# Slots of h of 2,304 bytes instead of 2,176, and two buffers instead of three for two working tiles

## The chip, the core and the metric

The kernel runs on one core of one Trainium2 chip. The metric is the device time of one execution in microseconds (us); times are given as the median of several executions. Engines are named as in the profile: PE (TensorE) multiplies, PEld is its loading of the stationary operand, DVE (VectorE) and ACT (ScalarE) work on elements, POOL (GpSimd) does little here, SP issues the transfers.

## What is computed

One block of a streaming encoder, for 256 frames of 2048 channels in float32: two half-step feed-forward layers (FFN, 5504 channels) around a mixer of attention and pooling, each conditioned on a vector c, then a last norm. Cut to what matters here:

```python
mod = silu(c) @ w_ada + b_ada                 # nine vectors of 2048
sh1, sc1, g1, sh2, sc2, g2, sh3, sc3, g3 = split(mod, 9)
h = rmsnorm(x, ffn1_norm_g) * (1 + sc1) + sh1
a, b = split(h @ ffn1_w_in, 2)
x = x + 0.5 * g1 * ((silu(a) * b) @ ffn1_w_out)
h = rmsnorm(x, mix_norm_g) * (1 + sc2) + sh2
q, k, v, f, u = split(h @ w_in, ...)
x = x + g2 * (concat(attention(q, k, v, f), pool(u)) @ w_out)
h = rmsnorm(x, ffn2_norm_g) * (1 + sc3) + sh3
a, b = split(h @ ffn2_w_in, 2)
x = x + 0.5 * g3 * ((silu(a) * b) @ ffn2_w_out)
return rmsnorm(x, final_norm_g)
```

## The kernel before, in words

Channels lie on the 128 partitions, frames along them: x is 16 tiles (k = 0 to 15) of 128 x 256. Each float32 operand of a product is split into a high and a low part of type fp32r, and a product is three matmuls, high x high, high x low, low x high. `mm3` issues them for one weight tile of 128 x 128: L242 (wh with the high half of h, g or mix), L243 (wh with the low half), L244 (wl with the high half). The weights are the loaded operand, 256 columns of h, g or mix the moving one. I call these three a triple. In the projections of q, k and v (`project`, L768) it is the other way round: h is loaded, and the weights move.

**Weights** come in pieces of eight tiles (`load_piece`: 512 KB, five buffers raw). ACT copies a piece to wh in two halves (L193, `split_high`), DVE subtracts to wl (L203, `split_low`); there are four wh and three wl buffers, in turn. The pieces' order is the order in which PE uses the tiles, and it is written out by `next_piece`, which for each piece also lets the work beside it go on by one step: it splits the next piece, loads one further, adds a rate to a credit (`RATE0`: 0.36 per piece for the first 50, then `RATE1`: 0.40 while scales and shifts of a norm are next, 0.33 otherwise) and, at a credit of 1, loads one of the 144 rows of w_ada (1 MB, L109), which DVE multiplies with silu(c) and sums (L112). Its `step_chains` takes one step of each chain put off with `later`.

**h.** `make_h` builds tile k of a norm's output: DVE writes x * a * row into a working tile hu (L307), ACT adds the shift and writes the high half of h (L311), DVE writes the low half from hu and the high one (L314). The tile is 128 x 2 x 256 elements, high half first. `make_raw` builds a tile hraw of x * a without the row, of 2 x 258 elements used out of 2 x 272, for the products that start before the norm's root is known: pool tiles 6 and 7 and the first three visits' halves of the second FFN (`raw_of`).

**Stages.** `ffn_in` goes over 43 pairs of output tiles in visits: a visit takes one pair and all h tiles that are ready and not yet used for it, one PSUM half after the other. The first visit of the second FFN takes three pairs (`GROUP`), with k outermost, so that 18 matmuls in a row read one h tile. `residual_out` multiplies g (43 tiles) or mix (16 tiles), and adds to x. Between the FFNs stand the pool tiles (`pool_tile`), the projections and the attention.

**Working tiles touched by the change**, all 128 x 256 float32 or less: the ring "hu" (hu, and guess and rest of a norm's root in `rms_row`), three buffers, and the ring "act" (sq in `Stats.add`, L272; silu in `swiglu`, L383; junk in `norm_heads`, L783), three buffers.

**Where the tiles lie.** The built program gives each tile an address in bytes within a partition. The ring "h" has 16 slots, each of the size of its largest tile, hraw: 2 x 272 x 4 = 2,176 bytes. Slot n begins at 29,440 + 2,176 n: for even n a multiple of 256, for odd n 128 beyond one. The low half of h lies 1,024 bytes further, with the same remainder. In the ring "h" also lie the squares at the start (sq4) and the outputs at the end (ys). The ring "pair" follows, from 64,256, with 43 slots of 2,048 bytes: g, mix, pooled, spill and the attention's tiles; all begin at a multiple of 256 (remainder 768 of 1,024). Then come ada, raw and the weight parts: their halves begin 64 bytes beyond a multiple of 256, but for one half of every fourth wh tile (128 beyond, `BEHIND`) and all of every third wl tile (192 beyond). In the first visit of the second FFN, k = 0 to 7 lie in slots 11, 10, 15, 14, 13, 9, 12 and 0.

The order of DVE, ACT, PE and SP is written by hand (`manual_schedule`): an engine does its instructions in the order in which the program issues them.

Of the kernel before, what the change touches and what calls it, by code (L numbers as in the profile page):

```python
# [10 lines left out]
F32 = mybir.dt.float32  # L11
F32R = mybir.dt.float32r
# [4 lines left out]
P = 128  # L17
SEQ = 256
# [5 lines left out]
HD = 128  # L24
# [23 lines left out]
NEG = -3.0e38  # L48
GAP = 16
BEHIND = {"wh": (0, 0, 0, 2 * GAP), "wl": (0, 0, 0)}  # L50
WARM = 9
QSCALE = float(HD) ** -0.5

# [12 lines left out]
def block_kernel(ctx, tc, order, xT, cvec, wada, wts, wf, vecs, out):  # L66
# [5 lines left out]
    big = ctx.enter_context(tc.tile_pool(name="big", bufs=1))  # L72
    wpool = ctx.enter_context(tc.tile_pool(name="wpool", bufs=1))
    work = ctx.enter_context(tc.tile_pool(name="work", bufs=2))
# [3 lines left out]
    def mm_tile():  # L78
        return psum.tile([P, 512], F32, tag="mm", name="mm", bufs=4)

    def sm_tile():
        return psum.tile([P, 512], F32, tag="sm", name="sm", bufs=4)

    def pair_tile(shape, dt, name):
        return big.tile(shape, dt, tag="pair", name=name, bufs=43)
# [55 lines left out]
    def later(*steps):  # L141
        chains.append(list(steps))

    def step_chains(most=None):

        if most is None:
            for c in chains:
                c.pop(0)()
            chains[:] = [c for c in chains if c]
        else:  # L150
            while len(chains) > most:
                for f in chains.pop(0):
                    f()
# [20 lines left out]
    def part_tile(kind):  # L174

        behind = BEHIND[kind]
        i = turns[kind] % len(behind)
# [69 lines left out]
    def inverse_root(r, v, n, guess, rest):  # L247


        def first():  # L250
            nc.scalar.activation(guess, v, AF.Abs_reciprocal_sqrt, scale=1.0 / n, bias=eps_t)

        def newton():
            nc.vector.scalar_tensor_tensor(out=rest, in0=v, scalar=n * EPS, in1=guess, op0=ALU.add, op1=ALU.mult)
            nc.vector.scalar_tensor_tensor(out=rest, in0=rest, scalar=-0.5 / n, in1=guess, op0=ALU.mult, op1=ALU.mult)
            nc.vector.scalar_tensor_tensor(out=r, in0=rest, scalar=1.5, in1=guess, op0=ALU.add, op1=ALU.mult)

        return first, newton

    class Stats:  # L260
# [6 lines left out]
        def add(self, d):  # L267
            t = {}

            def square():  # L270
                t["sq"] = work.tile([P, SEQ], F32, tag="act", name="sq", bufs=3)
                nc.scalar.activation(t["sq"], x[d], AF.Square)  # L272

            def total():
                if d == KD - 1:
                    self.last = t["sq"]
                elif self.acc is None:
                    self.acc = work.tile([P, SEQ], F32, tag="gf", name="acc", bufs=3)
                    nc.vector.tensor_copy(out=self.acc, in_=t["sq"])
                else:  # L280
                    nc.vector.tensor_add(out=self.acc, in0=self.acc, in1=t["sq"])

            later(square, total)
            if d == KD - 1:
                step_chains(0)

        def rms_row(self, meanwhile=None, between=None):

            st = sm_tile()
            parts = self.parts or (self.acc, self.last)  # L290
            for i, part in enumerate(parts):
                nc.tensor.matmul(st[:, :SEQ], lhsT=ones, rhs=part, start=i == 0, stop=i == len(parts) - 1)  # L292
            self.row = work.tile([P, SEQ], F32, tag="rrow", name="rrow", bufs=1)
            guess, rest = (work.tile([P, SEQ], F32, tag="hu", name=n, bufs=3) for n in ("guess", "rest"))
            first, newton = inverse_root(self.row, st[:, :SEQ], D, guess, rest)
            first()
            if between:
                between()
            newton()
            if meanwhile:  # L300
                meanwhile()
            return self.row

    def make_h(d, rrow, a_col, b_col):

        u = work.tile([P, SEQ], F32, tag="hu", name="hu", bufs=3)
        nc.vector.scalar_tensor_tensor(out=u, in0=x[d], scalar=a_col, in1=rrow, op0=ALU.mult, op1=ALU.mult)  # L307
        h = big.tile([P, 2, SEQ], F32R, tag="h", name="h", bufs=16)

        def high():  # L310
            nc.scalar.activation(h[:, 0, :], u, AF.Identity, bias=b_col)  # L311

        def low():
            nc.vector.scalar_tensor_tensor(  # L314
                out=h[:, 1, :], in0=u, scalar=b_col, in1=h[:, 0, :].bitcast(F32), op0=ALU.add, op1=ALU.subtract
            )

        return h, high, low

    def make_raw(d, a_col, b_col):  # L320

        h = big.tile([P, 2, SEQ + 16], F32R, tag="h", name="hraw", bufs=16)[:, :, : SEQ + 2]
        b2 = b_col.to_broadcast([P, 2])

        def high():
            nc.scalar.activation(h[:, 0, :SEQ], x[d], AF.Copy, scale=a_col)
            nc.scalar.copy(out=h[:, 0, SEQ:], in_=b2)

        def low():
            nc.vector.scalar_tensor_tensor(  # L330
                out=h[:, 1, :SEQ], in0=x[d], scalar=a_col, in1=h[:, 0, :SEQ].bitcast(F32),
                op0=ALU.mult, op1=ALU.subtract,
            )
            nc.vector.tensor_sub(out=h[:, 1, SEQ:], in0=b2, in1=h[:, 0, SEQ:].bitcast(F32))

        return h, high, low
# [40 lines left out]
    def swiglu(ab, j, g):  # L377

        t = {}

        def act():
            t["s"] = work.tile([P, SEQ], F32, tag="act", name="silu", bufs=3)
            nc.scalar.activation(t["s"], ab[:, :SEQ], AF.Silu)  # L383

        def product():
            t["g"] = work.tile([P, SEQ], F32, tag="gf", name="gf", bufs=3)
            nc.vector.tensor_mul(out=t["g"], in0=ab[:, SEQ:512], in1=t["s"])
            g[j] = pair_tile([P, 2, SEQ], F32R, f"g{j}")

        def high():  # L390
            nc.scalar.copy(out=g[j][:, 0, :], in_=t["g"])

        def low():
            nc.vector.tensor_sub(out=g[j][:, 1, :], in0=t["g"], in1=g[j][:, 0, :].bitcast(F32))

        return act, product, high, low
# [100 lines left out]
    def modulated(s_sc, s_sh, v_norm, rrow_of, n_raw=0):  # L497
# [5 lines left out]
        def begin_raw(k):  # L503
            c = slice(k, k + 1)
            raw_h[k], *steps = make_raw(k, scales[s_sc][:, c], shifts[s_sc][:, c])
            rest["raw", k] = steps
            later(lambda: go_on(("raw", k), 1), lambda: go_on(("raw", k), 0))
# [19 lines left out]
        def start(k, wait=True):  # L527
            c = slice(k, k + 1)
            begun_h[k], high, low = make_h(k, rrow_of(), scales[s_sc][:, c], shifts[s_sc][:, c])
            if wait:  # L530
                slow.add(k)
                rest[k] = [high, low]
                later(lambda: None, lambda: go_on(k, 1), lambda: go_on(k, 0))
            else:
                high()
                rest[k] = [low]
# [92 lines left out]
    idle = mm_tile()  # L629
    for _ in range(WARM):  # L630
        nc.tensor.matmul(idle[:, :SEQ], lhsT=ones, rhs=x[0], start=True, stop=True)
# [142 lines left out]
    def norm_heads(pts, name):  # L774
        qr = [pair_tile([P, 4, HD], F32, f"qr{name}{tt}") for tt in range(2)]
        ss = work.tile([P, 8], F32, tag="ss", name="ss")
        r, guess, rest = (work.tile([P, 8], F32, tag=n, name=n) for n in ("rs_r", "rs_guess", "rs_rest"))

        def squares(tt):
            nc.scalar.copy(out=qr[tt], in_=pts[tt].rearrange("p (a b) -> p a b", a=4))  # L780
            for i in range(4):
                junk = work.tile([P, HD], F32, tag="act", name="junk", bufs=3)
                nc.scalar.activation(  # L783
                    junk, qr[tt][:, i, :], AF.Square, accum_out=ss[:, tt * 4 + i : tt * 4 + i + 1]
                )

        def scale(tt):
            for i in range(4):
                nc.scalar.activation(
                    qr[tt][:, i, :], qr[tt][:, i, :], AF.Copy, scale=r[:, tt * 4 + i : tt * 4 + i + 1]  # L790
                )

        later(lambda: squares(0), lambda: squares(1), *inverse_root(r, ss, HD, guess, rest), lambda: scale(0), lambda: scale(1))
        return qr
# [300 lines left out]
```

## Time and profile before

| what | value |
|---|---|
| median of 3 runs | 1770.55 us (1770.16 to 1771.66) |
| the profiled execution | 1770.31 us, its span 1768.6 us |
| busy: PE, PEld | 1753.8 us (99%), 1743.8 us (99%) |
| busy: DVE, ACT | 1371.4 us (78%), 922.2 us (52%) |
| read from HBM | 476.24 MB, 270 GB/s over the span |
| first FFN, products with h | 19 to 504 us |
| first FFN, products with g | 504 to 740 us |
| pool tiles 6 and 7, projections, attention | 740 to 905 us |
| pool tiles with h, attention | 905 to 948 us |
| products with mix | 948 to 1038 us |
| second FFN, raw tiles, then h | 1040 to 1521 us |
| second FFN, products with g | 1521 to 1756 us |

The span runs from the first to the last instruction; the execution's own time lies 1.7 us above it. A matmul's duration in the rows is the time from its start to its modelled end; matmuls overlap, so their pace is the distance from start to start: for a line of code, its last start less its first, over its count less one. A slice of 50 us shows how many matmuls overlap it (x430), how long each engine was busy in it, the granted clock and what the DMA engines moved.

### The profile page before, as it was taken

What the parts mean: (1) busy time and instruction counts of PE and PEld (TensorE: products, weight loads), DVE (VectorE), ACT (ScalarE), POOL (GpSimd) and SP (SyncE); (2) the same over time, 40 slices, a digit from 0 to 9 for tenths busy, and PEclk for the clock granted to TensorE, in tenths of its full rate; (3) what the DMA queues carried; (4) which work ended last, traced back from release to release, by engine and by line L of the source; (5) the groups of instructions that cost most, each with busy time, mean ns of one, the idle gap of its engine ahead of it and who ended that gap; (6) DMA issues with size and microseconds to landing.
All of it is one profiled execution on the core that took longest, in us unless ns stands there. A gap on an engine that the chain in (4) does not pass through costs nothing.

```text
span 1768.6 us, 37313 instructions
## 1 busy us (share of the span) xinstructions
PE 1753.8 (99%) x14966; PEld 1743.8 (99%) x14966; DVE 1371.4 (78%) x2390; ACT 922.2 (52%) x1871; POOL 8.3 (0%) x54
## 2 busy tenths in 40 slices
PE   9999999999999999999999999999999999999997
PEld 7999999999999999999999999999999999999997
DVE  7899889999988888797989998777765555555554
ACT  7644445555554444477766555544444444544442
POOL 0000000000000000100000000000000000000000
PEclk9999999999999999999999999999999999999999
DMA  9889898888889989767966977877775555555553
GB/s 367 317 319 331 319 339 316 309 308 314 311 319 335 328 329 334 286 237 301 344 223 248 330 285 249 296 268 259 262 258 189 189 188 191 191 191 192 194 195 112
DMA packets 111937, 480.79 MB, mean 272 GB/s; under 512 B 12425, under 2 KB 12689, under 8 KB 93329
## 3 DMA queue, kind: packets, MB, share of 16 engines
q1 hardware_dynamic: 111762, 478.39, 75.4%
q8 instruction: 117, 1.92, 0.4%
q14 instruction: 58, 0.48, 0.1%
HBM read 476.24 MB, written 2.11 MB: 270 GB/s over the span
## 4 chain that ended last, share of the span: by engine, by line
PE 98%; ACT 1%; DMA 1%; DVE 0%; issue 0%; SPq 0%; DVEq 0%
PE mm L243 30%; PE mm L242 29%; PE mm L244 29%; PE mm L768 8%; DMA ada<-in_wada 1%; ACT wh L193 0%; ACT spill L454 0%; DVE y L1029 0%; PE sm L802 0%; PE sm L832 0%; PE sm L881 0%; PE sm L872 0%; PE sm L292 0%; PE sm L699 0%; PE sm L701 0%
## 5 line engine op out<-in xcount | busy, mean ns | idle before, releaser
L193 ACT CAST wh<-raw 128x512 fp32r<-128x512 f32 x1228 | 701.2, 620 | 725.1 <-PE mm L243 442.0
L203 DVE TENSOR_TENSOR wl<-raw,wh 128x512 fp32r<-128x512 f32 x1228 | 788.2, 686 | 319.0 <-issue 285.2
L242 PE MATMUL mm<-h,wh 128*128 128x256 f32 x2800 | 782.1, 279 | 0.8 <-ACT h L311 0.4
L243 PE MATMUL mm<-h,wh 128*128 128x256 f32 x2800 | 782.8, 280 | 0.1
L244 PE MATMUL mm<-h,wl 128*128 128x256 f32 x2800 | 781.9, 279 | 0.0
L242 PEld LDWEIGHTS mm<-h,wh 128*128 128x128 f32 x2800 | 526.3, 188 | 2.0 <-ACT spill L454 1.0
L243 PEld LDWEIGHTS mm<-h,wh 128*128 128x128 f32 x2800 | 525.8, 188 | 0.4 <-DVE h L314 0.3
L244 PEld LDWEIGHTS mm<-h,wl 128*128 128x128 f32 x2800 | 526.0, 188 | 0.0
L244 PE MATMUL mm<-g,wl 128*128 128x256 f32 x1376 | 380.8, 277 | 0.0
L243 PE MATMUL mm<-g,wh 128*128 128x256 f32 x1376 | 380.5, 277 | 0.0
L242 PE MATMUL mm<-g,wh 128*128 128x256 f32 x1376 | 380.5, 276 | 0.0
L112 DVE SCALAR_TENSOR_TENSOR ada<-ada,crow 128x2048 f32<-128x2048 f32 x144 | 329.2, 2286 | 23.5 <-DMA ada<-in_wada 22.9
L243 PEld LDWEIGHTS mm<-g,wh 128*128 128x128 f32 x1376 | 258.4, 188 | 0.0
L244 PEld LDWEIGHTS mm<-g,wl 128*128 128x128 f32 x1376 | 258.4, 188 | 0.0
L242 PEld LDWEIGHTS mm<-g,wh 128*128 128x128 f32 x1376 | 258.3, 188 | 0.0
L768 PE MATMUL mm<-wh,h 128*128 128x256 f32 x768 | 137.3, 282 | 0.0
L768 PEld LDWEIGHTS mm<-wh,h 128*128 128x128 f32 x768 | 117.4, 188 | 0.5 <-issue 0.2
L768 PE MATMUL mm<-wl,h 128*128 128x256 f32 x384 | 107.2, 279 | 0.0
L768 PEld LDWEIGHTS mm<-wl,h 128*128 128x128 f32 x384 | 72.3, 188 | 0.0
L244 PE MATMUL mm<-mix,wl 128*128 128x256 f32 x256 | 70.9, 277 | 0.0
L243 PE MATMUL mm<-mix,wh 128*128 128x256 f32 x256 | 70.8, 277 | 0.0
L242 PE MATMUL mm<-mix,wh 128*128 128x256 f32 x256 | 70.8, 277 | 0.0
(166 smaller groups left out, 1002.9 us busy)
## 6 DMA issues: line engine op xcount, KB each, us to landing
raw<-in_wts SPq DMA_DIRECT2D x614, 512.0 KB, 4.4
ada<-in_wada SPq DMA_DIRECT2D x144, 1024.0 KB, 7.6
x<-in_xT SPq DMA_DIRECT2D x4, 512.0 KB, 5.5
out<-y SPq DMA_DIRECT2D x8, 256.0 KB, 2.2
fb<-frow_d SPq DMA_DIRECT2D x4, 256.0 KB, 8.0
vec<-in_vecs SPq DMA_DIRECT2D x1, 109.5 KB, 10.1
wfc<-in_wf SPq DMA_DIRECT2D x1, 64.0 KB, 5.7
crow<-in_cvec SPq DMA_DIRECT2D x1, 8.0 KB
```

Source lines behind the costliest of these rows:

```text
L112: nc.vector.scalar_tensor_tensor(out=r, in0=r, scalar=1.0, in1=crow, op0=ALU.mult, op1=ALU.mult, accum_out=mod[section][:, t : t + 1],)
L193: nc.scalar.copy(out=wh[i], in_=raws[0][:, i * HALF : (i + 1) * HALF])
L203: nc.vector.tensor_sub(out=wl[i], in0=raw[:, i * HALF : (i + 1) * HALF], in1=wh[i].bitcast(F32))
L242: nc.tensor.matmul(out_ap, lhsT=wh, rhs=hk[:, 0, :], start=start, stop=False, skip_group_check=shared)
L243: nc.tensor.matmul(out_ap, lhsT=wh, rhs=hk[:, 1, :], start=False, stop=False, skip_group_check=shared)
L244: nc.tensor.matmul(out_ap, lhsT=wl, rhs=hk[:, 0, :], start=False, stop=stop, skip_group_check=shared)
L768: nc.tensor.matmul(pts[tt][:, c], lhsT=lhs, rhs=rhs[:, c], start=k == 0 and not half and not i, stop=k == KD - 1 and i == 2, skip_group_ch ...
```

## The change

`h_slot` gives every tile h and hraw the same room of 576 elements, 2,304 bytes, nine times 256. The low half of h stays 1,024 bytes behind the high one; that of hraw moves from 1,088 to 1,152 bytes behind it. The rings "hu" and "act" go from three buffers to two. Of the 16 x 128 bytes that the slots take more, and the 2 x 1,024 bytes that the two rings take less, nothing is left over.

```diff
+SLOT = 576
...
-                t["sq"] = work.tile([P, SEQ], F32, tag="act", name="sq", bufs=3)
+                t["sq"] = work.tile([P, SEQ], F32, tag="act", name="sq", bufs=2)
...
-            guess, rest = (work.tile([P, SEQ], F32, tag="hu", name=n, bufs=3) for n in ("guess", "rest"))
+            guess, rest = (work.tile([P, SEQ], F32, tag="hu", name=n, bufs=2) for n in ("guess", "rest"))
...
+    def h_slot(name, half):
+
+        return big.tile([P, SLOT], F32R, tag="h", name=name, bufs=16)[:, : 2 * half].rearrange("p (a b) -> p a b", a=2)
+
     def make_h(d, rrow, a_col, b_col):
 
-        u = work.tile([P, SEQ], F32, tag="hu", name="hu", bufs=3)
+        u = work.tile([P, SEQ], F32, tag="hu", name="hu", bufs=2)
         nc.vector.scalar_tensor_tensor(out=u, in0=x[d], scalar=a_col, in1=rrow, op0=ALU.mult, op1=ALU.mult)
-        h = big.tile([P, 2, SEQ], F32R, tag="h", name="h", bufs=16)
+        h = h_slot("h", SEQ)
...
     def make_raw(d, a_col, b_col):
 
-        h = big.tile([P, 2, SEQ + 16], F32R, tag="h", name="hraw", bufs=16)[:, :, : SEQ + 2]
+        h = h_slot("hraw", SEQ + P // 4)[:, :, : SEQ + 2]
...
-            t["s"] = work.tile([P, SEQ], F32, tag="act", name="silu", bufs=3)
+            t["s"] = work.tile([P, SEQ], F32, tag="act", name="silu", bufs=2)
...
-                junk = work.tile([P, HD], F32, tag="act", name="junk", bufs=3)
+                junk = work.tile([P, HD], F32, tag="act", name="junk", bufs=2)
```

In the built program slot n of "h" now begins at 29,440 + 2,304 n, a multiple of 256 for every n. "pair" begins at 66,304, and every tile behind it lies 2,048 bytes further than before, up to the end of the ring "act", behind which nothing moves. On every engine the instructions stand in the same order as before. What differs is what some wait for: 24 of the 48 writes of hu wait for a later instruction of DVE than before or for one at all, and 34 of ACT's on sq, silu and junk for one of ACT.

## Rows read from the trace of the kernel before

**Rows 1.** The page: busy time per engine, granted clock, chain that ended last.
```profile
PE 1753.8 (99%) x14966; PEld 1743.8 (99%) x14966; DVE 1371.4 (78%) x2390; ACT 922.2 (52%) x1871; POOL 8.3 (0%) x54
...
PEclk9999999999999999999999999999999999999999
...
PE 98%; ACT 1%; DMA 1%; DVE 0%; issue 0%; SPq 0%; DVEq 0%
```

**Rows 2.** PE's longest wait: <- releaser: us in total, times, longest.
```profile
PE mm L600 <- DMA crow<-in_cvec: 2.5, 1, 2.5
```

**Rows 3.** PE on h, two stretches: xcount: ns min/median/max, first and last start.
```profile
L242 PE MATMUL mm<-h,wh x1333: 276/279/290, 36.0 to 503.8; 128*128 128x256 f32 x191
...
L242 PE MATMUL mm<-h,wh x1328: 274/279/284, 1055.8 to 1520.9; 128*128 128x256 f32 x190
```

**Rows 4.** PE on tiles g (526:726) and mix (956:1036), the same view.
```profile
L242 PE MATMUL mm<-g,wh x586: 276/276/284, 525.8 to 725.8; 128*128 128x256 f32 x196
...
L244 PE MATMUL mm<-mix,wl x235: 276/276/285, 955.8 to 1035.8; 128*128 128x256 f32 x118
```

**Rows 5.** PE's timeline, second FFN's first visit: each slot's first matmul (start).
```profile
1057.90 0.28 PE L242 MATMUL mm<-h,wh 128*128 128x256 f32 x1
...
1059.95 0.28 PE L242 MATMUL mm<-h,wh 128*128 128x256 f32 x1
...
1062.04 0.28 PE L242 MATMUL mm<-h,wh 128*128 128x256 f32 x1
...
1064.16 0.28 PE L242 MATMUL mm<-h,wh 128*128 128x256 f32 x1
...
1066.31 0.28 PE L242 MATMUL mm<-h,wh 128*128 128x256 f32 x1
...
1068.43 0.28 PE L242 MATMUL mm<-h,wh 128*128 128x256 f32 x1
...
1070.55 0.28 PE L242 MATMUL mm<-h,wh 128*128 128x256 f32 x1
...
1072.66 0.28 PE L242 MATMUL mm<-h,wh 128*128 128x256 f32 x1
```

**Rows 6.** Timeline of PE where the stage of g begins.
```profile
504.46 0.28 PE L242 MATMUL mm<-g,wh 128*128 128x256 f32 x1
...
507.64 0.28 PE L242 MATMUL mm<-g,wh 128*128 128x256 f32 x1
...
508.67 0.28 PE L242 MATMUL mm<-g,wh 128*128 128x256 f32 x1
```

**Rows 7.** Stretches: us, busy PE, PEld, DVE, ACT, POOL (x), PEclk, DMA, GB/s.
```profile
76.00:126.00 50.00, 50.00 (x430) 50.00 (x429) 48.32 (x80) 22.41 (x41) 0.00 (x0) 1.00 0.90 319
...
226.00:276.00 50.00, 50.00 (x430) 50.00 (x429) 45.40 (x73) 24.65 (x45) 0.00 (x0) 1.00 0.92 333
526.00:576.00 50.00, 50.00 (x441) 50.00 (x440) 43.01 (x78) 23.43 (x46) 0.00 (x0) 1.00 0.92 333
```

**Rows 8.** DVE: ada from 226 to 276 us, hu, a piece of the chain.
```profile
L112 DVE SCALAR_TENSOR_TENSOR ada<-ada,crow 128x2048 f32<-128x2048 f32 x7 | 16.0, 2287 | 3.7 <-DMA ada<-in_wada 3.7
...
L307 DVE SCALAR_TENSOR_TENSOR hu<-x,a,rrow x48: 474/480/487, 18.2 to 1111.0; 128x256 f32<-128x256 f32 x48
...
1759.30 0.02 issue
1759.33 0.43 DVE rest L255
```

**Rows 9.** PE on h (904:948), on hraw, and line L768: xcount: ns.
```profile
L242 PE MATMUL mm<-h,wh x96: 276/279/467, 904.9 to 947.0; 128*128 128x256 f32 x96
...
L243 PE MATMUL mm<-hraw,wh x80: 279/283/386, 739.9 to 1055.5; 128*128 128x258 f32 x80
...
L768 PE MATMUL mm<-wh,h x768: 274/279/476, 752.3 to 904.7; 128*128 128x256 f32 x192
L768 PE MATMUL mm<-wl,h x384: 276/279/292, 752.5 to 904.8; 128*128 128x256 f32 x192
```

## The prediction

> **What bounds the kernel now.** I read the page's busy times first: PE is busy for 1753.8 of 1768.6 us, its granted clock is at its full level (2.4 GHz) in every slice, and the chain that ended last is PE for 98% [rows 1]. The list of PE's waits comes next: its longest entry is 2.5 us, once, at the start [rows 2]. So PE hardly ever waits for another engine, and only two things can move the time: the number of matmuls, which the change leaves alone, or the pace at which one matmul follows another. A triple is the three matmuls of one weight tile (L242, L243, L244, 256 columns each). Its pace follows from first start, last start and count of one line. In the first FFN's input stage 1333 triples take 467.8 us, 351.2 ns each; in the second FFN's, 1328 take 465.1 us, 350.5 ns [rows 3]. In the stages that read g and mix the same three instructions take 200.0 us for 585 intervals (g), or 80.0 us for 234 (mix), which is 341.9 ns [rows 4]. Shape, type, weights and clock are the same; h costs 8.6 to 9.3 ns more per triple. What differs is where the moving operand starts: all g and mix tiles begin at a multiple of 256 bytes, of h every second slot begins 128 bytes beyond one.
>
> **Does the address make the difference?** The first visit of the second FFN keeps one h tile for 18 matmuls, slot after slot [rows 5]. Slot 10 (even, aligned) takes 2.05 us, 342 ns per triple. Slot 15 takes 2.09, slot 13 takes 2.15, slot 9 takes 2.12 us (odd; 348, 358 and 353 ns). But slots 14, 12 and 0 (even) take 2.12, 2.12 and 2.11 us, the slow pace too. So there are two paces, about 342 and about 353 ns per triple, and an aligned operand allows the fast one without forcing it. The stage of g shows how a slow stretch ends. It inherits the slow pace from h: the first nine triples of g take 3.18 us, 353 ns each, then three take 1.03 us [rows 6], and from 526 us on the average is 341.9 [rows 4]. Nothing else happened there than that aligned tiles followed each other over several weight pieces. With h as it is, an odd slot comes after almost every even one, so the slow pace is renewed each time; 351 is what a mixture of 342 and 353 or more gives.
>
> The Trainium skill speaks against this change. Its page TensorE: Matmul & The Clock Gate (Part 2: What happens when you issue a matmul) says that the moving operand and the weight load have independent read ports, so that loading the next weights takes nothing from the running matmul, and gives a gap of N/2.4 + 2.5 ns. By that an estimate from the page is 109 ns per matmul, 328 ns per triple, at any address, and the change would be worth nothing. The rows disagree: 350.5 and 341.9 ns for equal instructions at one clock [rows 3, 4].
>
> **The change, part by part.**
> 1. Slots of 2,304 bytes from the same first address: every h tile then starts at a multiple of 256, its low half 1,024 further, also a multiple. I take the pace of g and mix for h, as the row of the same instructions on tiles that are all aligned. First FFN: 1333 x (351.2 - 341.9) = 12.4 us. Second: 1328 x (350.5 - 341.9) = 11.4 us. The six later pool tiles have 96 triples of h [rows 9]; at 8.6 ns that is 0.8 us. Sum 24.6 us, all on PE and so on the path. Bounds: upward 24.6 us, since no stage of the trace runs this triple faster than 341.9; downward a loss, in the rivals.
> 2. Slow stretches that remain after PE has waited or after the raw tiles: the one of rows 6 lasted nine triples at 11 ns, 0.1 us. I allow six of them, 0.6 us.
> 3. The cover. With PE faster, DVE has less time for each weight piece. Between 76 and 126 us it is busy for 48.3 of 50 us; the same pieces at 341.9 instead of 351.2 would come in 48.7 us, so it just fits. From 226 to 276 us it is busy for 45.4, with DMA at a share of 0.92 and 333 GB/s [rows 7], and waits 3.7 us for rows of ada [rows 8]. In the stage of g DMA had the same share and rate, at the faster pace of PE [rows 7]. But in the stage of h the rate of ada is 0.40 per piece once 50 pieces are through, against 0.36, so some waits may reach PE: between 0 and half of the first FFN's gain, 6 us. I take 1 us, since the wl tiles are made ahead by up to two pieces and the next stage ran at that pace without a wait.
> 4. Two buffers for hu. The instructions of every engine keep their order; only waits differ. 24 of the 48 writes of hu (480 ns each [rows 8]) now wait for a later instruction of DVE itself, nearly always the last before them that read the old tile. Such a wait on its own engine shows as the 0.02 us of "issue" between the dependent instructions of the last root [rows 8]: 24 x 0.02 = 0.5 us of DVE, beside PE. Queued behind are splits of weights, covered as in 3. If that cover were gone it would be 0.5 us on the path; I take 0.
> 5. Two buffers for sq, silu and junk. 34 instructions of ACT get or change a wait on ACT itself, at the same price 0.7 us of an engine that is busy for 52% [rows 1]: 0.
> 6. The raw tiles: their low half now starts 1,152 bytes behind the high one, 128 beyond a multiple of 256, while the high half is aligned. 80 triples [rows 9] at plus or minus 11 ns are within 0.9 us; before, none of their low halves was aligned either. I take 0.
> 7. The projections (L768) have the weights as moving operand, at addresses that keep their remainder, and h as the loaded one. Of 1152 matmuls [rows 9] half load an odd slot; bounds are 0 and 576 x 11/3 ns = 2.1 us. I take 0, since the moving side doesn't change.
> All that lies behind the h slots moves by 2,048 bytes, eight times 256, which costs nothing.
> Sum: 24.6 - 0.6 - 1.0 = 23.0 us. The profiled execution took 1770.31 us (the median of the runs is 0.24 us higher): **1747.3 us**.
>
> **The rivals.**
> *Only the odd slots gain.* They come to what an even slot gives today, and the even ones stay. With odd triples at 353 [rows 5] and a mean of 350.9 over both stages, even ones stand at 348.8; with 354 they stand at 347.8. 1400 odd triples times 4.2 to 6.2 ns is 6 to 9 us: 1762 to 1764 us. For it: slots 12 and 0 follow each other, both even, and stay slow [rows 5]. Against it: rows 6, and 200 us of g at the fast pace.
> *The slow pace locks in (slower).* Mechanism: h slots now alternate between the two halves of 512 bytes, where all g tiles have one remainder; if that keeps every stretch at the pace of slots 14, 12 and 0, all 2757 triples of h take 353.3 ns (2.12 us for six [rows 5]) instead of 350.9, which is 6.6 us more: 1777 us. It decides as soon as over (350.9 - 341.9) / (353.3 - 341.9) = 79% of the triples are slow. For it: three even slots at that pace for all their 18 matmuls [rows 5]. Against it: slot 10 has the other remainder of 512 than g, and both run at 342 [rows 4, 5].
> *Address has no part in it.* h differs from g by something else (two halves of a PSUM tile in turn, a visit's order). Then only waits on an engine's own work are left, and it stays within 0.2%, about what a measurement of this kernel can tell from no change (3.5 us): 1770 us. For it: the even slots 14, 12 and 0 are as slow as odd ones [rows 5]. Against it: slot 10 runs at 342 in the same stage with the same halves. The rule of the Trainium skill's page TensorE: Matmul & The Clock Gate (Part 2) would give this rival's time.
> *DVE becomes the bound in the first FFN* and gives back 6 us (part 3): 1752 us.
>
> **How the numbers follow.** Full gain 0.70, DVE or ada in the way 0.06, odd slots alone 0.13, no part of the address 0.06, lock 0.05. The first two lie between 1745 (24.6 us, and 0.7 of part 7 or the raw tiles) and 1753. The range reaches on to 1762 to take in the better half of the odd-slot case, 0.82 in all. Faster by over 0.2%: 0.70 + 0.06 + 0.13 = 0.89; the same 0.06; slower 0.05.
>
> **What would show it.** Right: line L242 on h between 1126 and 1326 us shows about 585 triples instead of 571, median duration 276 instead of 279; the g stages keep 341.9; PE's waits stay at a few us; DVE between 76 and 126 us is over 98% busy. Wrong: a median of 281 on h would be the lock; 278 or 279 with some 575 triples only the odd slots; new waits of PE for wl (L203) or ada the bound on DVE. A different pace of g would say that the pace is not a matter of the moving tile's address.

## The result, and the profile after

The change makes the kernel faster: the median is 1750.84 us (1750.21 to 1751.68), that of the kernel before on the same chip 1770.40 us (1770.16 to 1771.66). The ratio is 0.9888, with an interval of 0.9871 to 0.9906. That is 19.6 us less, where 23.0 us were forecast. The profiled execution took 1751.68 us, its span 1750.0 us, 18.6 us less than that of before.

Lines have moved by 1 to 5: a triple is now L243, L244 and L245, the writing of wl L204, the sum of an ada row L113, the projections L773. The page of the kernel after, with the lines of [rows 1]:

```profile
PE 1732.9 (99%) x14966; PEld 1721.5 (98%) x14966; DVE 1371.0 (78%) x2390; ACT 921.1 (53%) x1871; POOL 8.3 (0%) x54
...
PEclk9999999999999999999999999999999999999999
...
PE 96%; DMA 1%; DVE 1%; ACT 1%; issue 0%; SPq 0%; DVEq 0%; ACTq 0%
```

The same matmuls, the same work of DVE and ACT, the same granted clock. But PE's share of the chain that ended last has fallen by two points, and DVE, which had 0%, stands in it with 1%. PE's waits of the kernel after, to be read against [rows 2] (releaser: us in total, times, longest):

```profile
PE mm L605 <- DMA crow<-in_cvec: 2.6, 1, 2.6
PE mm L245 <- DVE wl L204: 1.9, 3, 1.0
```

The first entry is the old one. The second is new: three times PE waited for a low part of the weights. PEld's list of the same kernel has five such waits:

```profile
PEld mm L245 <- DVE wl L204: 3.1, 5, 1.1
```

PE on the tiles h, g and raw, and the projections (xcount: duration in ns min/median/max, first and last start), in the order first FFN, second FFN, 200 us of the second FFN, pool tiles, g, raw, projections; to be read against [rows 3, 4, 9]:

```profile
L243 PE MATMUL mm<-h,wh x1336: 276/276/383, 35.6 to 495.8; 128*128 128x256 f32 x191
...
L243 PE MATMUL mm<-h,wh x1328: 276/276/284, 1048.7 to 1502.4; 128*128 128x256 f32 x190
...
L243 PE MATMUL mm<-h,wh x586: 276/276/284, 1126.0 to 1325.9; 128*128 128x256 f32 x196
...
L243 PE MATMUL mm<-h,wh x96: 274/276/469, 897.9 to 939.4; 128*128 128x256 f32 x96
...
L243 PE MATMUL mm<-g,wh x586: 276/276/284, 525.9 to 725.9; 128*128 128x256 f32 x196
...
L243 PE MATMUL mm<-hraw,wh x80: 277/282/472, 731.4 to 1048.3; 128*128 128x258 f32 x80
...
L773 PE MATMUL mm<-wh,h x768: 274/280/471, 743.9 to 897.7; 128*128 128x256 f32 x192
```

Last start less first, over count less one: the second FFN's 1327 intervals take 453.7 us, 341.9 ns per triple, where they took 350.5. The first FFN's 1335 take 460.2 us, 344.7 ns, where they took 351.2 [rows 3]. g stands where it stood, 200.0 us for 585 intervals [rows 4]. The projections take 153.8 us from first to last start, where they took 152.4 [rows 9].

Where the 18.6 us of span come from, stage by stage: first FFN on h 1332 x (351.2 - 344.7) = 8.7; second FFN 465.1 - 453.7 = 11.4; pool tiles 42.1 - 41.5 = 0.6. Against it stand the projections with 1.4, the stretch of raw tiles ahead of the second FFN (18.2 us from the last matmul on mix to the first on h, now 18.8) with 0.6, and the start (first matmul on h 0.5 us later). That is 18.2 of 18.6 us.

Three stretches of the kernel after, with the columns of [rows 7], show the first FFN's loss:

```profile
76.00:126.00 50.00, 49.89 (x437) 49.69 (x437) 47.50 (x78) 22.35 (x41) 0.00 (x0) 1.00 0.88 317
...
226.00:276.00 50.00, 48.95 (x427) 48.56 (x427) 45.27 (x71) 24.39 (x45) 0.00 (x0) 1.00 0.92 337
526.00:576.00 50.00, 50.00 (x441) 50.00 (x440) 44.14 (x80) 24.39 (x49) 0.00 (x0) 1.00 0.94 339
```

From 226 to 276 us only 427 matmuls of PE overlap the slice, fewer than the 430 of before; the stage of g has 441. DVE is not full there (45.27 of 50 us); it waits. DVE's wait from 120 to 276 us, and the landing of an ada row over the whole program (KB each, median us from issue to landing):

```profile
DVE ada L113 <- DMA ada<-in_wada: 12.6, 12, 2.0
```

```profile
ada<-in_wada SPq DMA_DIRECT2D x144, 1024.0 KB, 7.7
```

The timeline of the kernel after around one of these waits (start, duration, engine, line; in brackets the idle time before it and its releaser):

```profile
237.55 2.29 DVE L113 SCALAR_TENSOR_TENSOR ada<-ada,crow 128x2048 f32<-128x2048 f32 x1 [1.98 <-DMA ada<-in_wada]
...
240.66 0.28 PE L244 MATMUL mm<-h,wh 128*128 128x256 f32 x1
...
241.15 1.89 DVE L204 TENSOR_TENSOR wl<-raw,wh 128x512 fp32r<-128x512 f32 x3
...
241.89 0.39 PE L245 MATMUL mm<-h,wl 128*128 128x256 f32 x1 [0.95 <-DVE wl L204]
```

DVE works in the order of issue. It stood 1.98 us before a row of ada, so the split of wl queued behind that row came late, and PE stood 0.95 us before its next matmul.

### The profile page after: what moved, and what is told of

It is laid out like the page before. It is cut to its first block, busy times and chain, and to the rows that moved or that the text cites. A ratio compares the mean times of both kernels' runs of the same rounds, so it can differ in the third digit from the quotient of the medians.

```text
span 1750.0 us, 37330 instructions
## 1 busy us (share of the span) xinstructions
PE 1732.9 (99%) x14966; PEld 1721.5 (98%) x14966; DVE 1371.0 (78%) x2390; ACT 921.1 (53%) x1871; POOL 8.3 (0%) x54
## 4 chain that ended last, share of the span: by engine, by line
PE 96%; DMA 1%; DVE 1%; ACT 1%; issue 0%; SPq 0%; DVEq 0%; ACTq 0%
PE mm L245 29%; PE mm L243 29%; PE mm L244 29%; PE mm L773 8%; DMA ada<-in_wada 1%; DVE wl L204 0%; ACT wh L194 0%; ACT spill L459 0%; DVE y L1034 0%; PE sm L886 0%; PE sm L807 0%; PE sm L837 0%; DVE ada L113 0%; PE sm L877 0%; PE sm L293 0%
## 5 line engine op out<-in xcount | busy, mean ns | idle before, releaser
L204 DVE TENSOR_TENSOR wl<-raw,wh 128x512 fp32r<-128x512 f32 x1228 | 786.9, 686 | 295.7 <-issue 265.0
L245 PE MATMUL mm<-h,wl 128*128 128x256 f32 x2800 | 775.5, 277 | 2.1 <-DVE wl L204 1.9
L243 PE MATMUL mm<-h,wh 128*128 128x256 f32 x2800 | 775.3, 277 | 0.5 <-ACT spill L459 0.5
L244 PE MATMUL mm<-h,wh 128*128 128x256 f32 x2800 | 774.6, 277 | 0.1
L245 PEld LDWEIGHTS mm<-h,wl 128*128 128x128 f32 x2800 | 525.8, 188 | 3.1 <-DVE wl L204 3.1
L243 PEld LDWEIGHTS mm<-h,wh 128*128 128x128 f32 x2800 | 525.6, 188 | 1.7 <-ACT spill L459 1.1
L244 PEld LDWEIGHTS mm<-h,wh 128*128 128x128 f32 x2800 | 525.7, 188 | 0.4 <-DVE h L319 0.3
L245 PE MATMUL mm<-g,wl 128*128 128x256 f32 x1376 | 380.7, 277 | 0.0
L244 PE MATMUL mm<-g,wh 128*128 128x256 f32 x1376 | 380.5, 277 | 0.0
L243 PE MATMUL mm<-g,wh 128*128 128x256 f32 x1376 | 380.4, 276 | 0.0
L113 DVE SCALAR_TENSOR_TENSOR ada<-ada,crow 128x2048 f32<-128x2048 f32 x144 | 329.3, 2287 | 30.9 <-DMA ada<-in_wada 30.4
L245 PEld LDWEIGHTS mm<-g,wl 128*128 128x128 f32 x1376 | 258.4, 188 | 0.0
L244 PEld LDWEIGHTS mm<-g,wh 128*128 128x128 f32 x1376 | 258.3, 188 | 0.0
L243 PEld LDWEIGHTS mm<-g,wh 128*128 128x128 f32 x1376 | 258.3, 188 | 0.0
L773 PE MATMUL mm<-wh,h 128*128 128x256 f32 x768 | 138.8, 283 | 0.0
L773 PEld LDWEIGHTS mm<-wh,h 128*128 128x128 f32 x768 | 117.7, 188 | 0.5 <-issue 0.2
L773 PE MATMUL mm<-wl,h 128*128 128x256 f32 x384 | 107.3, 279 | 0.0
L773 PEld LDWEIGHTS mm<-wl,h 128*128 128x128 f32 x384 | 72.1, 188 | 0.0
L245 PE MATMUL mm<-mix,wl 128*128 128x256 f32 x256 | 70.9, 277 | 0.0
L244 PE MATMUL mm<-mix,wh 128*128 128x256 f32 x256 | 70.8, 277 | 0.0
L243 PE MATMUL mm<-mix,wh 128*128 128x256 f32 x256 | 70.8, 277 | 0.0
```

Source lines behind the costliest of these rows:

```text
L113: nc.vector.scalar_tensor_tensor(out=r, in0=r, scalar=1.0, in1=crow, op0=ALU.mult, op1=ALU.mult, accum_out=mod[section][:, t : t + 1],)
L204: nc.vector.tensor_sub(out=wl[i], in0=raw[:, i * HALF : (i + 1) * HALF], in1=wh[i].bitcast(F32))
L243: nc.tensor.matmul(out_ap, lhsT=wh, rhs=hk[:, 0, :], start=start, stop=False, skip_group_check=shared)
L244: nc.tensor.matmul(out_ap, lhsT=wh, rhs=hk[:, 1, :], start=False, stop=False, skip_group_check=shared)
L245: nc.tensor.matmul(out_ap, lhsT=wl, rhs=hk[:, 0, :], start=False, stop=stop, skip_group_check=shared)
L773: nc.tensor.matmul(pts[tt][:, c], lhsT=lhs, rhs=rhs[:, c], start=k == 0 and not half and not i, stop=k == KD - 1 and i == 2, skip_group_ch ...
```

## The experiments

Each is compared with the kernel before on the same chip. The edits are to the kernel after, unless they say "to the kernel before".

**Two buffers alone.** To the kernel before: the five tiles of the rings "hu" and "act" with two buffers, and an unused tile of 2,048 bytes ahead of the slots, so that what lies behind the slots lies where it does after the change, and the slots keep their remainders.

```diff
-        u = work.tile([P, SEQ], F32, tag="hu", name="hu", bufs=3)
+        u = work.tile([P, SEQ], F32, tag="hu", name="hu", bufs=2)
...
+    big.tile([P, 512], F32, name="fill", bufs=1)
```

> The kernel before with two buffers for hu and act instead of three, the slots of h as before (2,176 bytes, every second one 128 beyond a multiple of 256), and an unused tile of 2,048 bytes ahead of them, so that everything behind lies as in the changed kernel. Address theory (the start of the moving operand sets the pace): a triple of h in the second FFN stays at 350 to 351 ns, the time is that of before within 0.2%, 1767 to 1774 us. Rival (the gain comes from the rings or from where the other tiles lie): a triple below 346 ns, under 1762 us.

Measured: 1772.54 us against 1772.12, ratio 1.0005 (0.9996 to 1.0014): no difference. h in the second FFN is as slow as in the kernel before (in this run a triple is L242 to L244):

```profile
L243 PE MATMUL mm<-h,wh x571: 276/279/285, 1125.8 to 1325.7; 128*128 128x256 f32 x191
```

So the buffers and the shift by 2,048 bytes give no part of the gain that can be told, and cost at most 2.5 us (0.0014 of the time); the gain lies with the slots.

**Tiles of odd k 128 bytes further.** Slots as after the change, but in those of every odd k the tile begins 128 bytes into its slot.

```diff
-        return big.tile([P, SLOT], F32R, tag="h", name=name, bufs=16)[:, : 2 * half].rearrange("p (a b) -> p a b", a=2)
+        return big.tile([P, SLOT], F32R, tag="h", name=name, bufs=16)[:, at : at + 2 * half].rearrange("p (a b) -> p a b", a=2)
...
-        h = h_slot("h", SEQ)
+        h = h_slot("h", SEQ, 32 * (d % 2))
...
```

Here and in the next run the low half of a raw tile also lies 1,088 bytes behind its high half again.

> The changed kernel with its slots and rings, but tiles of odd k begin 128 bytes further within their slot: only the alignment is undone. Address theory: a triple of h in the second FFN is back at 350 to 351 ns (stage from 454 to 465 us), PE's waits for wl in the first FFN are gone (its h stage about 484 us), the projections are back near 152.6 us; 1767 to 1774 us. Rival (the slots' size or the rings make the pace): 341.9 ns, 1748 to 1754 us.

Measured: 1777.03 us against 1772.12, ratio 1.0029 (1.0018 to 1.0040), slower than before, and 3 us above the range expected. h in the second FFN:

```profile
L243 PE MATMUL mm<-h,wh x567: 277/281/290, 1125.8 to 1325.9; 128*128 128x256 f32 x189
```

200.1 us for 566 intervals, 353.5 ns per triple. With the same slots and the same buffers the whole gain is gone: it is the start of the tile that counts. In the kernel before two slots of one kind follow each other now and then [rows 5]; here the kinds alternate with every k, and the median duration is 281, not 276.

**All tiles of h 128 bytes further.**

```diff
-        return big.tile([P, SLOT], F32R, tag="h", name=name, bufs=16)[:, : 2 * half].rearrange("p (a b) -> p a b", a=2)
+        return big.tile([P, SLOT], F32R, tag="h", name=name, bufs=16)[:, 32 : 32 + 2 * half].rearrange("p (a b) -> p a b", a=2)
...
```

> The changed kernel with every tile of h 128 bytes further within its slot. Address theory: each triple of h at the slow pace, 353 to 354 ns, the second FFN's h stage 469 to 470 us, in all 1774 to 1782 us. Rival (what costs is the change of remainder from one tile to the next, not the remainder): 341.9 to 343 ns and 1748 to 1756 us.

Measured: 1762.15 us against 1772.12, ratio 0.9948 (0.9934 to 0.9961), in neither of the two ranges.

```profile
L243 PE MATMUL mm<-h,wh x579: 276/276/283, 1126.0 to 1325.9; 128*128 128x256 f32 x193
```

199.9 us for 578 intervals, 345.8 ns. Here my reading fell: not one tile begins at a multiple of 256, and more than half of the gain is there. If every tile had its own price by its start, tiles half at 0 and half at 128 would cost (341.9 + 345.8) / 2 = 343.9 ns; the run before this one measured 353.5. So some 10 ns come from the start's change between one moving tile and the next.

The 4 ns by which this run's h is slower than that of the change are not a price that each triple pays. The starts show whole stretches at one pace or the other (PE's timeline, the first triple of each stretch and the first behind it):

```profile
1136.62 0.28 PE L243 MATMUL mm<-h,wh 128*128 128x256 f32 x1
...
1146.14 0.28 PE L243 MATMUL mm<-h,wh 128*128 128x256 f32 x1
...
1147.55 0.28 PE L243 MATMUL mm<-h,wh 128*128 128x256 f32 x1
...
1157.47 0.28 PE L243 MATMUL mm<-h,wh 128*128 128x256 f32 x1
```

By the addresses of the built program both stretches have all moving tiles at 128 and wh at 64 (of 256 bytes). The 28 triples of the first take 9.52 us, 340 ns each, the 28 of the second 9.92 us, 354 each. Between the two lie four triples on a piece of wh that begins at 128. From 1126 to 1326 us 339 of the 507 triples with wh at 64 take 340 ns, the others 354 on average. So tiles at 128 allow the fast pace as well; the difference lies in slow stretches that last.

**The loaded weights at the same remainder as h.** The gap of 64 bytes ahead of the weight tiles is put behind the third wh; three of the four wh and two of the three wl then begin at a multiple of 256, like h, g and mix.

```diff
-    wpool.tile([P, GAP], F32, name="gap", bufs=1)
...
+    wpool.tile([P, GAP], F32, name="gap", bufs=1)
     state["credit"] = CREDIT
```

> The changed kernel with the 64 unused bytes ahead of the weight parts put behind the third wh tile: three of four wh and two of three wl tiles now begin at a multiple of 256, as h, g and mix do. Theory of the moving operand alone: h, g and mix keep 341.9 ns per triple; the projections, whose moving operand the weights are, get faster by up to 4 us (1152 matmuls from 117.8 to 114 ns); 1746 to 1752 us. Rival (what counts is the distance of the two operands, 64 bytes in the fast stages): h, g and mix all fall to about 353 ns for most pieces, 4400 triples times 6 to 11 ns, 1777 to 1800 us.

Measured: 1812.23 us against 1772.12, ratio 1.0229 (1.0215 to 1.0243), beyond even the rival's range. h and g, in the same view (in this run a triple is L242 to L244):

```profile
L242 PE MATMUL mm<-h,wh x562: 276/283/287, 1125.9 to 1325.9; 128*128 128x256 f32 x188
...
L243 PE MATMUL mm<-g,wh x562: 274/283/283, 525.8 to 725.8; 128*128 128x256 f32 x188
```

200.0 us for 561 intervals, 356.5 ns, on h and g alike. So the moving tile's remainder of 0 is not fast as such: it is fast beside weights that begin 64 bytes off, and slowest of all beside weights most of which have the same remainder. The triples whose loaded tiles all begin at 0, half of all, take 360 ns on average.

Whether the distance of the two operands decides, or the loaded tile's own start (64 or 192 against 0 or 128), this run doesn't tell: in every run the moving tiles h, g and mix begin at 0 or 128. The projections of the kernel after speak against the distance alone. There h is loaded, at 0, and the weights move, at 64 in this stretch, so that the operands lie 64 bytes apart as well. PE's timeline, each third matmul (only wl's), the first and the last:

```profile
749.82 0.28 PE L773 MATMUL mm<-wl,h 128*128 128x256 f32 x1
...
755.12 0.28 PE L773 MATMUL mm<-wl,h 128*128 128x256 f32 x1
```

Fifteen times three matmuls take 5.30 us, 353 ns for three: the slow pace.

**Rows of ada used one piece later.** An ada row is summed four pieces after its load was issued, not three.

```diff
-LAG0, LAG = 1, 3
+LAG0, LAG = 1, 4
```

> The changed kernel, in which DVE sums a row of w_ada four weight pieces after its load was issued instead of three. Theory (the gain lost in the first FFN is lost where DVE stands at its head waiting for a row that has not landed: three pieces at 2.74 us are 8.2 us, and rows land 7.7 us after their issue, so that little is left, and DVE idled 12.6 us before L113 between 120 and 276 us): DVE's idle time before L113 there falls below 4 us, PE's waits for wl go, the h stage of the first FFN takes 473 to 474 us instead of 476.5; about 3 us faster than the changed kernel. Rival (the transfers as a whole are too slow at 0.40 rows per piece): the waits stay, and the time too.

Measured: 1748.75 us against 1771.87, ratio 0.9870 (0.9855 to 0.9885). The change itself was measured on another chip; by the two ratios this run is 3.2 us better, by the spans of the profiled executions (1747.0 against 1750.0 us) 3.0. The first FFN and the projections:

```profile
L245 PE MATMUL mm<-h,wl x1336: 276/276/285, 35.8 to 492.2; 128*128 128x256 f32 x191
...
L773 PE MATMUL mm<-wh,h x768: 274/280/471, 740.1 to 895.2; 128*128 128x256 f32 x192
```

The first FFN's 1335 intervals take 456.4 us, 341.9 ns: the 3.8 us that it lacked are there, and neither DVE's wait for ada from 120 to 276 us nor PE's for wl is in the trace any more. The projections give 1.3 us back (155.1 against 153.8).

**The lower rate of ada for longer.**

```diff
-RATE0, N_RATE0 = 0.36, 50
+RATE0, N_RATE0 = 0.36, 100
```

> The changed kernel with the rate of 0.36 rows of w_ada per piece kept for 100 pieces instead of 50, and the lag of three pieces. Theory of the lag: each row still lands late, DVE's idle time before L113 falls only as the number of rows in the stretch does (by a tenth), 0 to 1.5 us are won. Rival (the transfers' rate is the limit, 345 GB/s asked where the stage of g asks for 330): the idle time more than halves and PE's waits for wl go, 2.5 to 3.5 us are won.

Measured: 1749.23 us against 1771.87, ratio 0.9873 (0.9859 to 0.9886). By the ratios that is 2.7 us better than the change, a time in the rival's range, and by the spans 2.0. But the waits are still there (DVE from 120 to 276 us, then PE), and the first FFN gains little (last row):

```profile
DVE ada L113 <- DMA ada<-in_wada: 11.5, 8, 2.0
...
PE mm L245 <- DVE wl L204: 1.3, 2, 0.9
...
L243 PE MATMUL mm<-h,wh x1336: 276/276/383, 35.7 to 494.5; 128*128 128x256 f32 x191
```

The first FFN takes 458.8 us where the change took 460.2: 1.4 us won, as the theory of the lag has it, of the 3.8 that one piece more brought back. Fewer rows in that stretch mean fewer late ones, and each is no less late (1.4 us on average against 1.05). The time allowed to a row is what was short.

**All of wh 64 bytes beyond a multiple of 256.** The second half of every fourth wh tile began at 128; now it begins where the others do.

```diff
-        return w[:, :HALF], w[:, HALF + behind[i] // 2 : UN + behind[i] // 2]
+        return w[:, :HALF], w[:, HALF : UN]
```

> The changed kernel with the second half of every fourth wh tile 64 bytes beyond a multiple of 256, as all the other halves, instead of 128 beyond (the tile keeps its room). Theory (what counts is the distance of the moving operand's start from the loaded one's, and 128 is a slow distance; a triple with wh at 128 takes 352 to 357 ns, the others 340): an eighth of some 4400 triples gains 12 to 17 ns, 7 us in all, of which the first FFN's half may be lost in waits for wl and ada; g and mix fall from 341.9 to about 340.3 ns per triple; 4 to 7 us faster than the changed kernel. Rival (the odd half serves to bring a slow stretch back to the fast pace): without it stretches of 353 ns that last, at least 5 us slower.

Measured: 1744.34 us against 1771.87, ratio 0.9845 (0.9832 to 0.9859), by the ratios 7.6 us better than the change. h in the second FFN, g, and PE's wait:

```profile
L243 PE MATMUL mm<-h,wh x589: 276/276/276, 1126.0 to 1326.0; 128*128 128x256 f32 x197
...
L243 PE MATMUL mm<-g,wh x589: 276/276/276, 526.0 to 726.0; 128*128 128x256 f32 x197
...
PE mm L245 <- DVE wl L204: 3.6, 4, 1.6
```

200.0 us for 588 intervals: 340.1 ns on h and g alike, and every duration is 276. With PE this much faster the late rows of ada cost more, 3.6 us of waits instead of 1.9.

**The same edit to the kernel before.**

> The kernel before with the same edit. Theory of the distance: g and mix fall to 340.3 ns per triple as in the changed kernel (4 us), h gains little since its odd slots renew the slow pace: 3 to 5 us faster than before. Rival (the odd half ends slow stretches): h gets slower, up to 354 ns per triple, and g keeps the 353 ns with which it begins until a third wl tile comes; within 2 us of before or slower.

Measured: 1764.98 us against 1771.87, ratio 0.9961 (0.9949 to 0.9974), 6.9 us where 3 to 5 were expected. g falls to 340.1 ns; h keeps its slow pace:

```profile
L242 PE MATMUL mm<-h,wh x573: 276/279/283, 1125.8 to 1325.7; 128*128 128x256 f32 x191
...
L242 PE MATMUL mm<-g,wh x589: 276/276/276, 525.9 to 725.9; 128*128 128x256 f32 x197
```

h takes 199.9 us for 572 intervals here, 349.5 ns, and about 1 ns less per triple over both FFNs, which is nearly as much in all as g and mix gain. The two edits add up (0.9888 x 0.9961 = 0.9849, both together 0.9845): one concerns the moving tiles, the other the loaded ones.

**Both: wh at 64 throughout, and the lag of four.**

> The changed kernel with both edits that were faster alone: the second half of every fourth wh tile 64 bytes beyond a multiple of 256, and four pieces of lag for the rows of w_ada. Theory: every triple of h, g and mix at 340 ns, no wait of PE for wl in the first FFN (its h stage 60.9 to 61 us and seven times 58.5, 470.5 us, instead of 477), the projections at 153.5 to 155.5 us; 1738 to 1741 us. Rival (at 340 ns DVE itself is the bound between 76 and 176 us, 48.3 of 50 us before): the lag wins only a part, 1742 to 1744 us, with waits of PE for wl left.

Measured: **1740.33 us** against 1771.76, ratio 0.9819 (0.9806 to 0.9832), the fastest version of this study. Both FFNs:

```profile
L243 PE MATMUL mm<-h,wh x1336: 276/276/383, 35.7 to 489.7; 128*128 128x256 f32 x191
...
L243 PE MATMUL mm<-h,wh x1328: 276/276/278, 1041.2 to 1492.4; 128*128 128x256 f32 x190
```

454.0 us for 1335 intervals and 451.2 for 1327: 340.1 and 340.0 ns. No wait for wl is left.

**The lag of four in the kernel before.**

> The kernel before with four pieces of lag for the rows of w_ada. Theory (late rows reach PE only when PE runs at the fast pace): no difference that can be told, 0.998 to 1.002 of before. Rival (they cost PE something before, too, in the executions at the upper end of its runs): 1 to 3 us faster than before, with less spread between its runs.

Measured: 1771.16 us against 1771.76, ratio 0.9995 (0.9986 to 1.0004): no difference. The first FFN and the projections:

```profile
L242 PE MATMUL mm<-h,wh x1335: 276/279/290, 35.8 to 503.7; 128*128 128x256 f32 x191
...
L768 PE MATMUL mm<-wh,h x768: 274/279/476, 751.9 to 905.4; 128*128 128x256 f32 x192
```

The first FFN takes 350.7 ns per triple instead of 351.2, some 0.6 us in all, and the projections lose 1.1 (153.5 us against 152.4), as they do in the changed kernel. At 351 ns per triple no wait for wl is in PE's list with either lag; it is the faster pace of the change that brought the late rows to the path.

## Why the prediction was right, and where it was off

**The slots (part 1)** carried the sum, and held to the decimal where nothing else interfered: 11.4 us on the second FFN as forecast, 586 triples in 200 us where about 585 were named, median 276, g unchanged; the pool tiles gave 0.6 us of the 0.8 reckoned. Taking the pace of g for h was sound because h now stands to the weights exactly as g does; for the same reason what was too narrow in the reason given did not show in the number.

**The reason given for it was too narrow.** The prediction put it that "an aligned operand allows the fast one without forcing it" and that "the slow pace is renewed each time". The second half is what the runs bear out: tiles in turn lose all of the gain (353.5). The first half falls: tiles all at 128 allow the fast pace too (340 ns for two thirds of the triples with wh at 64, 345.8 on average), and a remainder of 0 is the slowest of all beside weights at 0 (356.5).

What the runs show is this. The fast pace, 340 ns, came only in triples whose loaded tiles begin at 64 or 192 of 256 bytes: of those with a wh at 0 or 128, or a wl at 0, none in the kernel after and in the runs with h at 128 or without the gap took under 344 ns. And a slow pace of about 354 ns, once begun, goes on for a while with the starts unchanged. The kernel after shows it behind one of PE's waits, with moving tiles at 0 and wh at 64 (the matmul that waited, then the first triple behind it and the ninth):

```profile
123.76 0.39 PE L245 MATMUL mm<-h,wl 128*128 128x256 f32 x1
...
123.98 0.28 PE L243 MATMUL mm<-h,wh 128*128 128x256 f32 x1
...
126.81 0.28 PE L243 MATMUL mm<-h,wh 128*128 128x256 f32 x1
```

Eight triples take 2.83 us, 354 ns each, and then it is 340 again. The nine slow triples of [rows 6] are the same thing. By the addresses of the built program both stretches end at the first triples of a piece whose wl begins at 192 after one at 64, so that in [rows 6] something else did happen than aligned tiles following each other. In the run with all tiles at 128 a slow stretch outlasts such a piece; what begins and what ends one was not tried by itself, and stays open.

The pieces at 128 also explain the 341.9 ns which I took for the floor ("no stage of the trace runs this triple faster"): it was itself a mixture. The first visit of the second FFN in the kernel after shows the piece of wh that begins at 128, four triples in 32:

```profile
1063.73 0.28 PE L243 MATMUL mm<-h,wh 128*128 128x256 f32 x1
...
1065.14 0.28 PE L243 MATMUL mm<-h,wh 128*128 128x256 f32 x1
...
1065.48 0.28 PE L243 MATMUL mm<-h,wh 128*128 128x256 f32 x1
```

From 1063.73 to 1065.14 us four triples take 1.41 us, 352 ns each; the next takes 340. And (28 x 340 + 4 x 354) / 32 = 341.8, the old floor to a tenth, with 354 as the mean of such triples (352 ns with a low part at 64, 357 with one at 192).

**Slow stretches that remain (part 2),** 0.6 us taken: they come as forecast, and smaller. In the first FFN a dozen triples behind PE's waits take 350 to 358 ns, some 0.2 us too much in all; two follow the raw tiles in the second FFN.

**The cover (part 3) was the term that was mis-sized.** 1.0 us was taken, the first FFN lost 12.4 - 8.7 = 3.7 us, within the bound of 6. From start to start, the five triples in which the loading of wl waited took 3.5 us more than 340 ns each, and the slow triples behind them 0.2: that is the whole of it. The prediction saw the waits for ada and the rate of 0.40, and reasoned that wl tiles made ahead would hide them. What it left out is the deadline: three pieces of eight triples at 341.9 ns are 8.2 us, and a row lands in 7.7 in the median, so that half a microsecond is left, and a row slower than that holds DVE up: 12.6 us in 12 times from 120 to 276 us, where the kernel before had 9.6 us in 9, with no wait of PE for wl. With one piece more, 10.9 us, the 3.8 us came back; with fewer rows and the same deadline, only part. The stage of g, of which the prediction said that it "ran at that pace without a wait", has waits of DVE for ada too: 3.1 us in 5 times from 500 to 740 us in the kernel before, 7.0 us in 7 in the kernel after, without reaching PE. That DMA's share is the same in both stages [rows 7] said nothing on that.

The check named for DVE, over 98% busy from 76 to 126 us, did not come: it was 47.50 of 50 us. DVE never was full; it was made to wait. As a rival, "DVE becomes the bound" had the right place and the wrong mechanism.

**Two buffers (parts 4 and 5)** cost nothing that can be told, as taken; shown by the run with two buffers alone (ratio 1.0005).

**The raw tiles (part 6):** the stretch ahead of the second FFN took 0.6 us longer, within the 0.9 allowed to both sides. But with the same slots and buffers as after the change, where it took 18.8 us, it took 18.3 in the runs with rows used one piece later and with the lower rate; with those of before, where it took 18.2, it took 18.6 in the run with all of wh at 64. So single executions scatter by as much. The start, 19.2 us before, is at 19.7 in that last run too.

**The projections (part 7)** were taken at 0 with a gain of up to 2.1 us as the bound; they lost 1.4. The bound excluded a loss without a reason. Of their 1152 matmuls 1114 follow each other directly; these come at 116.5 ns from start to start before and at 117.8 after, which is the whole 1.4 us. The two runs with h at 128, all or in turn, took 152.9 and 153.0 us from first to last start, less than the 153.8 of the change, and the run without the gap 155.1. So the address of the loaded h has a part in it, but which relation is good there, where the weights move, stays open.

**The sum:** 23.0 forecast, 18.6 in the profiled executions. Of the 4.4 us missing, the first FFN has 3.7 - 1.0 - 0.6 = 2.1 beyond what was set aside for the cover and for slow stretches, the projections 1.4, the raw stretch 0.6, the start 0.5 and the pool tiles 0.2. These are 4.8; the 0.4 between lie in the stretches that are not listed.

**The rivals.** "Only the odd slots gain" is out: its 278 or 279 as median did not come. "The slow pace locks in" is out: 276 throughout. "Address has no part in it" is out, most plainly by the run without the gap: equal instructions, equal clock, and 1812 us there against 1744 with all of wh at 64, by starts of tiles alone. The Trainium skill's page TensorE: Matmul & The Clock Gate (Part 2: What happens when you issue a matmul) names no part of a start address in the pace. It has the next weights loaded through a read port of their own, which takes no read bandwidth from the running matmul, and its N/2.4 + 2.5 ns, which it calls the gap of an isolated matmul, gives an estimate of 109 ns. The runs have 113.3 ns per matmul (340.0 / 3) where the moving tiles begin at 0 and the weights at 64 or 192, and 118.8 (356.5 / 3) where most of both begin at 0, and the measurement decides. Whether the load takes something from the matmul, or is itself slower from some starts, no run here shows.

## What to carry to other kernels

Where matmuls follow each other back to back and loads of weights run beside them, look at the start address of the moving and of the loaded tiles, not at their size alone: in this kernel moving tiles that all begin at 0 of 256 bytes were worth 3.7% more beside weights at 64 or 192 than beside weights most of which begin at 0 too (1744 against 1812 us). Compare equal instructions of different stages by last start less first over the count: here a stage that was 2.5% slower at the same clock had a cause that no list of waits showed. And when the bound engine gets faster, recompute the deadline of every load that is counted in its pieces: here one piece more of lead was worth 3.8 us in its stage, of which the projections took back 1.3.

## What the runs showed of the hardware that was not expected

- The pace of a matmul of 256 columns depends on where both operands start. With the moving tile at 0 of 256 bytes a triple took 340 ns beside weights at 64 or 192, 352 or 357 beside a wh at 128, and 360 beside wh and wl at 0.
- With the same starts there are two paces, 340 and about 354 ns, and the slow one goes on for a while: eight triples behind a wait, 28 in the run with all moving tiles at 128.
- A moving start that goes to and fro between 0 and 128 costs some 10 ns per triple more than either start alone: 353.5 ns against 341.9 and 345.8. What in the chip does this no run here shows.
- PE's list of waits counts too little: it has 1.9 us in three waits for wl, PEld's has 3.1 in five, and from start to start the five took 3.5. A matmul's row lasts 276 ns where the next starts after 113, so that part of a wait lies under the row of the matmul before it.
